# A row-wise infinity norm: 29 tail loads down to 704 columns in place of 25 down to 1152, two memsets behind them, early stores on ScalarE's queue

## Chip, cores, metric

Every program runs on one core of a Trainium2 chip. Time is device time in microseconds (us), the median of several executions. "Span" is the profiled execution from its first to its last instruction; the time lies about 1.8 us above it. A transfer has "landed" when the last of the sixteen updates of its semaphore is in the trace.

## The reference

```python
x = np.random.randn(8192, 8192).astype(np.float32)
def reference(x):
    return np.linalg.norm(x, ord=np.inf, axis=1)    # the largest |x| of each row
```

256 MiB are read once, 32 KiB are written.

## The kernel before

23 "big" loads of 128 partitions x 16384 columns (two rows a partition) fill a ring of three buffers; VectorE takes the largest magnitude of each row. The last 18 rows of every partition, the tail, come in shrinking loads, so that VectorE is soon done once the last byte is there. A planner, working backwards from the end, sizes them with two cost lines: a load costs `LOAD[0]` us a column and `LOAD[1]` a load, a reduction `REDUCE` likewise. Rows cut into several pieces are put together by GpSimd, the last row by the last reduction itself, which reads the partial maxima behind its own piece.

```python
LOAD = (1.1775e-3, 0.075)
REDUCE = (1.0417e-3, 0.060)
ROWS = 18
FIRST = 1152          # the last load's columns, at most
SNAP = 0.7
IDLE = 6
...
            fit = int((lag + slack - REDUCE[1] * n) / REDUCE[0])   # what VectorE can do in time
...
    for i in range(IDLE):
        tc.keep_in_program_order(nc.vector.memset(idle[:, i : i + 1], 0.0))

    early = nc.sync.dma_start(              # the 46 results a partition of the big loads
        out=out[:split].rearrange("(p q) -> p q", p=P), in_=res_big.rearrange("p t r -> p (t r)")
    )
    out_tail = out[split:].rearrange("(p r) -> p r", p=P)        # 18 results: 72 bytes a partition
    middle = nc.sync.dma_start(out=out_tail[:, : ROWS - 2], in_=res_tail[:, : ROWS - 2])
    for store in (early, middle):
        tc.add_manual_dep(store.ins, pieces.last[-2].name, ...)   # wait for the second-last reduction
    ...                                                           # SyncE waits for GpSimd
    last = nc.sync.dma_start(out=out_tail[:, ROWS - 2 :], in_=res_tail[:, ROWS - 2 :])
```

So there are three stores: the early one writes 184-byte runs, one a partition; the middle one the first 64 bytes of each 72-byte stretch of the tail's output; the last one the remaining 8 bytes of each stretch. The memsets write single elements that nothing reads.

Of the kernel before, what the change touches and what calls it, by code (L numbers as in the profile page):

```python
# [11 lines left out]
SEMS = 8  # L12


LOAD = (1.1775e-3, 0.075)
REDUCE = (1.0417e-3, 0.060)
ROWS = 18
FIRST = 1152
SNAP = 0.7
GRAIN = 64  # L20

IDLE = 6


def tail_loads(n_cols, big):







    slack = 0.0
    lag = REDUCE[0] * FIRST + REDUCE[1]
    loads = []
    end = ROWS * n_cols

    def take(top, bottom, most):
        nonlocal slack
        w = 0  # L40
        n = 0
        while True:

            n += 1
            start = max(bottom, (top - 1) // n_cols * n_cols - (n - 1) * n_cols)
            fit = int((lag + slack - REDUCE[1] * n) / REDUCE[0])
            w = max(w, min(fit, top - start) // GRAIN * GRAIN)
            if fit <= top - start or start <= bottom:
                break
        w = max(GRAIN, min(w, most, top - bottom))  # L50
        row = (top - w + n_cols - 1) // n_cols * n_cols
        if top - row >= SNAP * w or (w == most and top > row):
            w = top - row
        n = (top - 1) // n_cols - (top - w) // n_cols + 1
        slack += (LOAD[0] - REDUCE[0]) * w + LOAD[1] - REDUCE[1] * n
        loads.append((top - w, w))
        return top - w

    ends = [take(end, end - n_cols, FIRST), take(end - n_cols, end - 2 * n_cols, n_cols)]
    for top, bottom in zip(ends, (end - n_cols, 0)):  # L60
        while top > bottom:
            top = take(top, bottom, big)
    return loads[::-1]
# [61 lines left out]
def kernel(  # L125
# [5 lines left out]
    nc = tc.nc  # L131
# [3 lines left out]
    tail = tail_loads(n_cols, R * n_cols)  # L135
    split = n_rows - ROWS * P
    n_big = split // (R * P)
# [8 lines left out]
    res_big = single.tile([P, n_big, R], f32)  # L146
    res_tail = single.tile([P, ROWS], f32)
    idle = single.tile([1, IDLE], f32)
    pieces = Pieces(tc, ring)
# [9 lines left out]
    for i, (start, w) in enumerate(tail):  # L159
        c = 0  # L160
        while c < w:
            row = (start + c) // n_cols
            n = min(w - c, (row + 1) * n_cols - start - c)
            parts.append((row, i, c, n))
            c += n
    of_row = [[q for q in parts if q[0] == row] for row in range(ROWS)]

# [4 lines left out]
    for row, own in enumerate(of_row):  # L172
        if row == ROWS - 1:
            spots[own[-1][1]] = at
# [13 lines left out]
    for i, (start, w) in enumerate(tail):  # L188
# [8 lines left out]
        )  # L197
        for row in range(ROWS - 1):
            if len(of_row[row]) > 1 and of_row[row][-1][1] == i:
                best = dst[of_row[row][0]]  # L200
                more = [dst[q] for q in of_row[row][1:]]
                while more:
# [3 lines left out]
                        out=to,  # L206
# [7 lines left out]
    tc.declare_fence(done.ins, group="loads")  # L214
    for i in range(IDLE):
        tc.keep_in_program_order(nc.vector.memset(idle[:, i : i + 1], 0.0))  # L216

    early = nc.sync.dma_start(
        out=out[:split].rearrange("(p q) -> p q", p=P), in_=res_big.rearrange("p t r -> p (t r)")
    )  # L220
    out_tail = out[split:].rearrange("(p r) -> p r", p=P)
    middle = nc.sync.dma_start(out=out_tail[:, : ROWS - 2], in_=res_tail[:, : ROWS - 2])
    for store in (early, middle):
        tc.add_manual_dep(
            store.ins,
# [40 lines left out]
```

## Time and profile before

| | before |
|---|---|
| median of 3 runs | 629.24 us (629.21 to 629.35) |
| span | 627.395 us |
| first load landed | 22.556 us |
| last load landed | 623.594 us |
| last reduction | 623.715 to 625.062 us |
| last store issued, landed | 625.089, 626.550 us |

The profile's list of DMA issues gives the three stores, with KB and us from issue to landing:

```profile
out_dram<-res_big SPq DMA_DIRECT2D x1, 23.0 KB, 1.5
out_dram<-res_tail SPq DMA_DIRECT2D x1, 8.0 KB, 1.7
out_dram<-res_tail SPq DMA_DIRECT2D x1, 1.0 KB, 1.5
```

The 1 KB store that ends the kernel takes 1.5 us (1.461 in the trace).

### The profile page before, as it was taken

To read this page: it belongs to the slowest core of one execution; us is meant where nothing else is said; L and a number is where in the kernel's file an instruction comes from. 1 tells how busy PE (TensorE), PEld (TensorE's weight loads), DVE (VectorE), ACT (ScalarE), POOL (GpSimd) and SP (SyncE) were. 2 spreads that over 40 slices of the span, in tenths; PEclk is the share of its full clock that TensorE was granted. 3 is DMA by queue.
4 is the path that set the end of the run, shared out by engine and by line. 5 is a ranking of instruction groups with operands and counts; after the bars stand their busy time and mean duration, and the time that the engine had idled before them with its cause. 6 is when DMAs were issued, how large, how long until landed. Compare 5 with 4: busy or idle time off the path is not lost.

```text
span 627.4 us, 170 instructions
## 1 busy us (share of the span) xinstructions
DVE 551.9 (88%) x62; POOL 2.9 (0%) x13
## 2 busy tenths in 40 slices
DVE  0588988889988889888898888988889899999998
POOL 0000000000000000000000000000000000000000
DMA  9999999999999999999999999999999999999997
GB/s 401 401 468 401 468 401 468 401 468 401 468 401 468 401 468 401 468 401 468 401 468 401 468 401 464 405 455 414 443 410 440 452 401 429 432 440 429 419 423 298
DMA packets 7345, 268.48 MB, mean 428 GB/s; under 512 B 1200, under 2 KB 1200, under 8 KB 1968
## 3 DMA queue, kind: packets, MB, share of 16 engines
q1 hardware_dynamic: 7344, 268.47, 99.3%
q14 instruction: 1, 0.01, 0.0%
HBM read 268.44 MB, written 0.03 MB: 428 GB/s over the span
## 4 chain that ended last, share of the span: by engine, by line
DMA 57%; DVE 42%; issue 0%; DVEq 0%; SPq 0%
DMA ring<-in_x_dram 57%; DVE res_big L108 22%; DVE parts L108 11%; DVE res_tail L108 8%; DVE ring L108 1%; DVEq L261 0%; SPq L90 0%; DVE idle L216 0%
## 5 line engine op out<-in xcount | busy, mean ns | idle before, releaser
L108 DVE TENSOR_REDUCE res_big<-ring 128x2 f32<-128x16384 f32 x23 | 396.1, 17220 | 69.4 <-DMA ring<-in_x_dram 69.4
L108 DVE TENSOR_REDUCE res_tail<-ring 128x1 f32<-128x8192 f32 (+1 forms) x10 | 78.9, 7944 | 2.1 <-DMA ring<-in_x_dram 2.1
L108 DVE TENSOR_REDUCE parts<-ring 128x1 f32<-128x3520 f32 (+17 forms) x19 | 69.8, 3735 | 1.7 <-DMA ring<-in_x_dram 1.7
L108 DVE TENSOR_REDUCE ring<-ring 128x1 f32<-128x1984 f32 (+3 forms) x4 | 7.7, 1975 | 0.0
L205 POOL TENSOR_SCALAR res_tail<-parts 128x1 f32<-128x1 f32 x8 | 2.3, 289 | 614.1 <-DVE parts L108 614.1
L205 POOL TENSOR_SCALAR parts<-parts 128x1 f32<-128x1 f32 x1 | 0.4, 354 | 7.0 <-DVE parts L108 7.0
L250 POOL MEMSET const-bfloat16-1.0<- 128x1 bf16 x1 | 0.1, 102 | 0.0
L250 POOL MEMSET const-uint8-127<- 128x1 uint8 x1 | 0.1, 101 | 0.0
L250 POOL MEMSET const-float32-0.0<- 128x1 f32 x1 | 0.1, 98 | 0.2 <-issue 0.2
L250 POOL MEMSET const-float32-1.0<- 128x1 f32 x1 | 0.1, 98 | 0.0
L216 DVE MEMSET idle<- 1x1 f32 x6 | 0.1, 59 | 0.0
## 6 DMA issues: line engine op xcount, KB each, us to landing
ring<-in_x_dram SPq DMA_DIRECT2D x3, 4096.0 KB, 41.9
ring<-in_x_dram SPq DMA_DIRECT2D x1, 7488.0 KB, 31.1
ring<-in_x_dram SPq DMA_DIRECT2D x1, 6368.0 KB, 35.4
ring<-in_x_dram SPq DMA_DIRECT2D x1, 5920.0 KB, 40.8
ring<-in_x_dram SPq DMA_DIRECT2D x1, 4800.0 KB, 32.8
ring<-in_x_dram SPq DMA_DIRECT2D x1, 3488.0 KB, 40.4
ring<-in_x_dram SPq DMA_DIRECT2D x1, 3104.0 KB, 39.2
ring<-in_x_dram SPq DMA_DIRECT2D x1, 2944.0 KB, 40.8
```

The source lines that it names most:

```text
L108: ins = self.nc.vector.tensor_reduce(out=dst, in_=src, axis=mybir.AxisListType.X, op=mybir.AluOpType.max, apply_absolute_value=True,)
L205: combined = nc.gpsimd.tensor_scalar(out=to, in0=best, scalar1=two[0], scalar2=two[1] if len(two) == 2 else None, op0=mybir.AluOpType.max, ...
L216: tc.keep_in_program_order(nc.vector.memset(idle[:, i : i + 1], 0.0))
L250: nc = _bacc.Bacc("TRN2", target_bir_lowering=False, num_devices=1)
```

## The change

The intent: a smaller last piece leaves VectorE less to do after the last byte; 0.08 us are held back at each piece so that VectorE isn't late for it; and since the second-last reduction then ends only about 0.8 us before the last, the two early stores move to ScalarE's queue, out of the last store's way.

```diff
-LOAD = (1.1775e-3, 0.075)
+LOAD = (1.1775e-3, 0.073)
+SPARE = 0.08
-FIRST = 1152
-SNAP = 0.7
+FIRST = 768
+SNAP = 0.6
-IDLE = 6
+IDLE = 2
+        spare = SPARE if loads else 0
-            fit = int((lag + slack - REDUCE[1] * n) / REDUCE[0])
+            fit = int((lag + slack - spare - REDUCE[1] * n) / REDUCE[0])
-    early = nc.sync.dma_start(
+    early = nc.scalar.dma_start(
-    middle = nc.sync.dma_start(out=out_tail[:, : ROWS - 2], in_=res_tail[:, : ROWS - 2])
+    middle = nc.scalar.dma_start(
+        out=out_tail[:, : ROWS - 2], in_=res_tail[:, : ROWS - 2]
+    )
```

`FIRST` is only a cap. With 768 the planner's division comes out a hair under 768, and cut down to its grain of 64 columns that makes 704.

## The prediction

> **What bounds the kernel now.** I read the page first, then the timeline and the waits of the last microseconds, then three stretches of the tail.
>
> ```profile
> span 627.4 us, 170 instructions
> DVE 551.9 (88%) x62; POOL 2.9 (0%) x13
> DMA  9999999999999999999999999999999999999997
> q1 hardware_dynamic: 7344, 268.47, 99.3%
> HBM read 268.44 MB, written 0.03 MB: 428 GB/s over the span
> ...
> ring<-in_x_dram SPq DMA_DIRECT2D x1, 576.0 KB, 14.3
> ```
>
> The load queue is the bound: its packets fill 99.3% of 16 engines' span, and all 40 slices but the last read 9. VectorE works 88% of the span and is the follower. What can be won is the time between the last byte and the end, plus what every separate load costs the queue. The last line is the last load (1152 columns, 128 partitions, 4 bytes: 576 KB): it landed 14.3 us after its issue, so the queue held work and did not wait for issues.
>
> Next the waits of VectorE and the timeline from 615 us on (start, duration, what):
>
> ```profile
> DVE res_big L108 <- DMA ring<-in_x_dram: 69.4, 23, 22.6
> DVE parts L108 <- DMA ring<-in_x_dram: 1.7, 1, 1.7
> ```
>
> ```profile
> 622.32 1.47 DVE L108 TENSOR_REDUCE parts<-ring 128x1 f32<-128x1280 f32 x1
> 623.72 1.35 DVE L108 TENSOR_REDUCE res_tail<-ring 128x1 f32<-128x1156 f32 x1
> 623.82 0.35 SPq L218 DMA_DIRECT2D out_dram<-res_big  x1
> 623.97 0.28 POOL L205 TENSOR_SCALAR res_tail<-parts 128x1 f32<-128x1 f32 x1 [8.68 <-DVE parts L108]
> 624.21 0.43 SPq L222 DMA_DIRECT2D out_dram<-res_tail  x1
> 625.00 0.09 DVE L216 MEMSET idle<- 1x1 f32 x6
> 625.09 0.33 SPq L235 DMA_DIRECT2D out_dram<-res_tail  x1
> ```
>
> In the 23 big loads VectorE waits for each one. In the tail it waits once for 1.7 us (at 496.7 us) and never again: its reductions of shrinking pieces run back to back, a little behind the loads. The stretches say the same (us, busy and count by engine, clock, DMA share, GB/s):
>
> ```profile
> 564.00:600.00 36.00, 36.00 (x10) 1.12 (x4) 1.00 1.01 430
> 600.00:623.60 23.60, 23.60 (x11) 0.71 (x2) 1.00 0.97 404
> ```
>
> The trace's semaphore updates give the landings more finely than the page: the last load is complete at 623.594 us and the one before at 622.191. A reduction that finds VectorE free starts 0.024 us after the landing (22.556 to 22.580 for the first load). The last one started at 623.715, so it was 0.097 us late, behind VectorE's own work; the four before it were 0.09 to 0.11 us late too. The end is therefore: last landing 623.594, 0.121 to the start, 1.347 of reduction (to 625.062), 0.027 to the issue of the last store (625.089), 1.461 until that store has landed (626.550), and 0.845 of closing barriers to 627.395. The time of 629.24 lies 1.8 us over the span, which I take as fixed.
>
> **What the Trainium skill says.** "DMA: Bandwidth & Descriptors", section "Where 436 GB/s comes from", puts the ceiling of the 16 ports at 435.2 GB/s. I fitted the differences of the landings against the columns: 1.1764 ns a column plus 0.076 us a load, and all but the last load (0.028 us quicker) lie within 0.01 us of it. A column is 512 bytes, so the slope is 435.2 GB/s: the trace agrees, and the bytes cannot go faster; only the 0.076 us a load is open.
>
> "Perfetto Trace Analysis", section "Optimizing Scalar/DVE Operations", gives about 60 ns of overhead to a VectorE operation on SBUF and says that profiled latency is about twice this, since the write acknowledgement overlaps with the next instruction. The trace agrees: the step from the 1280-column reduction to the next is 1.394 us, that is 1.333 for 1280 columns at 1.0417 ns and 0.060 on top, while its listed duration is 1.474, 0.08 more.
>
> The DMA page's "Where the ~2 µs actually goes" puts most of a small transfer's fixed time into the write receipt. The last store's packets are over at 626.118 and its semaphore is full at 626.550, which fits. The same page's "Issuing engines are not separate DMA queues" says that another issuing engine saves only issue time. No run here shows that yet; I use it for ScalarE's stores.
>
> **The change, part by part.** I worked the new plan out with the fitted costs; the same arithmetic on the old plan puts the last reduction's end at 625.058 (measured 625.062).
>
> Four loads more (29 in place of 25), same bytes: 4 x 0.076 = +0.304 us on the bounding queue. The last landing goes from 623.594 to 623.898, keeping the 0.028 us that the last load was quicker.
>
> Smaller last piece: 704 columns and 6 partial maxima behind them, 710 elements in place of 1152 + 4 = 1156. 446 x 1.0417 ns = -0.465 us, so a duration of 0.882.
>
> The sparing term: the planner now takes 0.08 us off what VectorE may have at each piece behind the first, so that VectorE catches up. In my schedule the last reduction is 0.03 us late in place of 0.092 in the same model: -0.063 us. Sum at the end of the last reduction: 0.304 - 0.465 - 0.063 = -0.224, that is 624.83.
>
> The memsets, 6 to 2: the last store waits for the count that the last reduction gives, not for theirs. The semaphore's update comes 0.010 us after the reduction's end and the store starts 0.017 later, as after other reductions; the final update of the memsets comes at 625.128, after the store was issued. The page's wait of the last store for the memset is an inference from neighbouring times. Their updates are needed only at the closing drain, 1.5 us later: 0.00 us.
>
> The stores on ScalarE's queue: the second-last reduction (768 columns) should end at 624.03. Early and middle store, at their old distances from it, are issued at 624.06 and 624.45, the second taking 0.43 until 624.88. On SyncE that would hold up the last store, ready at 624.86, by some 0.05 us plus the instruction in between; on ScalarE it does not. So the move is worth nothing against before, and guards the 0.22 us of the rest. The middle store landed 1.72 us after its issue (624.214 to 625.933), so 626.17 now; the last one 624.86 + 1.461 = 626.32. The last store still ends last, by 0.15 us. The early store's packets would come at about 624.9, after the last load's 623.9, so they take nothing from the loads.
>
> Sum: 629.24 - 0.22 = 629.02.
>
> **The rivals.** First, the middle store becomes the end: its margin is 0.15 us. A first issue from ScalarE with 0.2 to 0.3 us more latency, or two stores side by side writing small runs into the same stretch of the output, would take it. For it: the middle store is already slower to land than the other two (1.72 against 1.47 and 1.46), and the two now start 0.4 apart in place of 0.875. Against it: their packets take only 0.2 us each. It would make 629.1 to 629.3.
>
> Second, VectorE stays behind: if each reduction costs 0.01 us more than I take, or the landings come a little sooner, the sparing term is eaten up over the last pieces, and the end is at the sum of reductions. That returns up to the 0.063, so 629.08. Against it: reductions of 1 to 2 thousand columns fit 1.0417 ns and 0.060 to 0.002 us.
>
> Third, the loads cost more when small: packets of 2816 bytes a partition in place of 4608. If the fixed cost of the five loads under 1280 columns were 0.1 in place of 0.076, the end moves by 0.12, to 629.14. Nothing in the loads down to 1280 columns hints at it; they keep the fit, and the 1152 one was quicker. If the missing 0.028 is a property of small loads and not of the last, the other four of these five would give 0.11 us more, and 628.91.
>
> **Range and chances.** All of these are tenths of a microsecond, 2% is 12.6. So "within 2%" is all but certain. I take 629.03, a shade above the sum for the first rival, and 628.86 to 629.28 as the range: from the friendly end of the third rival to the first rival at its worst. The spread of the three runs of before is 0.14 us, so a gain of 0.2 may be seen but hardly in a single run.
>
> **What would show it.** Last landing at 623.9; the last reduction of 710 elements lasting 0.88 and ending at 624.83; a start no more than 0.06 us behind its landing; small waits of VectorE for loads in the last ten pieces, where there were none; SyncE's last store issued 0.03 us after the reduction's end; ScalarE's middle store landing before it. I am wrong if the last landing is past 624.1 (loads dearer), if VectorE still shows no wait (spare eaten), or if the closing wait is ended by a ScalarE store.

## The result and the profile after

| | before | after |
|---|---|---|
| median, same rounds | 629.30 us (629.20 to 629.50, 6 runs) | 629.61 us (629.26 to 629.75, 6 runs) |
| ratio | | 1.0004, 95% interval 0.9991 to 1.0017 |

The ratio is the mean time of the changed kernel's fast runs over that of the other's of the same rounds, so it is not quite the ratio of the medians. "The same" by any 2% measure, as forecast, but the median lies 0.33 us above the top of the forecast range and on the other side of before: +0.31 where -0.22 was expected.

From the page after:

```profile
span 627.7 us, 175 instructions
q1 hardware_dynamic: 7632, 268.44, 99.3%
q10 hardware_dynamic: 288, 0.03, 0.0%
HBM read 268.44 MB, written 0.03 MB: 428 GB/s over the span
```

q10 is ScalarE's queue with the two early stores; the loads still fill 99.3%. The timeline from 622 us on answers the one in the prediction:

```profile
622.40 1.08 DVE L110 TENSOR_REDUCE ring<-ring 128x1 f32<-128x896 f32 x1
623.39 0.94 DVE L110 TENSOR_REDUCE parts<-ring 128x1 f32<-128x768 f32 x1
624.25 0.89 DVE L110 TENSOR_REDUCE res_tail<-ring 128x1 f32<-128x710 f32 x1
624.37 0.38 ACTq L220 DMA_DIRECT2D out_dram<-res_big  x1
624.51 0.36 POOL L207 TENSOR_SCALAR res_tail<-parts 128x1 f32<-128x1 f32 x1 [10.81 <-DVE parts L110]
624.79 0.51 ACTq L224 DMA_DIRECT2D out_dram<-res_tail  x1
625.08 0.06 DVE L218 MEMSET idle<- 1x1 f32 x2
625.16 0.35 SPq L239 DMA_DIRECT2D out_dram<-res_tail  x1
```

The last reduction takes 0.89 us, as computed, but ends at 625.14 where 624.83 was expected. The stores after, from the list of DMA issues:

```profile
out_dram<-res_big ACTq DMA_DIRECT2D x1, 23.0 KB, 2.1
out_dram<-res_tail ACTq DMA_DIRECT2D x1, 8.0 KB, 1.8
out_dram<-res_tail SPq DMA_DIRECT2D x1, 1.0 KB, 1.7
```

In this trace all three land more slowly than before, the deciding one by 0.2 us. And the very first reduction of the two traces (before, then after):

```profile
22.58 17.22 DVE L108 TENSOR_REDUCE res_big<-ring 128x2 f32<-128x16384 f32 x1 [22.58 <-DMA ring<-in_x_dram]
```

```profile
22.88 17.22 DVE L110 TENSOR_REDUCE res_big<-ring 128x2 f32<-128x16384 f32 x1 [22.88 <-DMA ring<-in_x_dram]
```

The same first load landed 0.30 us later, long before anything that the change touches. The difference of the spans, 627.678 - 627.395 = +0.283 us, is thus three pieces:

| piece | before | after | difference |
|---|---|---|---|
| first load's landing | 22.556 | 22.851 | +0.295 |
| from there to the end of the last reduction | 602.506 | 602.286 | -0.220 |
| from there to the end of the span ("tail" in the tables, not to be taken for the tail rows) | 2.333 | 2.541 | +0.208 |

The middle piece is what the prediction worked out (-0.224). The last one gives it back. The first needs a test: chance, or the price of a second queue?

### The profile page after: what moved, and what is told of

It reads as the page before. It is cut to its first block, busy times and chain, and to the rows that moved or that the text cites. A ratio compares the mean times of both kernels' runs of the same rounds, so it can differ in the third digit from the quotient of the medians.

```text
span 627.7 us, 175 instructions
## 1 busy us (share of the span) xinstructions
DVE 552.1 (88%) x62; POOL 3.2 (1%) x14
## 3 DMA queue, kind: packets, MB, share of 16 engines
q1 hardware_dynamic: 7632, 268.44, 99.3%
## 4 chain that ended last, share of the span: by engine, by line
DMA 57%; DVE 42%; issue 0%; DVEq 0%; SPq 0%
DMA ring<-in_x_dram 57%; DVE res_big L110 22%; DVE parts L110 12%; DVE res_tail L110 7%; DVE ring L110 1%; DVEq L265 0%; SPq L92 0%; DVE idle L218 0%
## 5 line engine op out<-in xcount | busy, mean ns | idle before, releaser
L110 DVE TENSOR_REDUCE parts<-ring 128x1 f32<-128x3136 f32 (+18 forms) x22 | 78.5, 3633 | 1.2 <-DMA ring<-in_x_dram 1.2
L110 DVE TENSOR_REDUCE res_tail<-ring 128x1 f32<-128x8192 f32 (+1 forms) x9 | 69.8, 7811 | 2.1 <-DMA ring<-in_x_dram 2.1
L110 DVE TENSOR_REDUCE ring<-ring 128x1 f32<-128x1600 f32 (+5 forms) x6 | 8.3, 1444 | 0.0
```

The costliest lines, as they stand in the source:

```text
L110: ins = self.nc.vector.tensor_reduce(out=dst, in_=src, axis=mybir.AxisListType.X, op=mybir.AluOpType.max, apply_absolute_value=True,)
```

## The experiments

Theory A: the gain at the last reduction is real and is given back because the last store lands slowly when other stores are close in front of it; the late start is chance. Theory B: using ScalarE's queue delays the start of the load stream. Rivals C (two queues at once make the receipts slow) and D (the plan of 29 loads, or the two memsets, do) came with them.

Fifteen kernels were run, each with five timed runs beside nine of before, and one trace. In the table, F is the first load's landing, R the end of the last reduction; "last store" is from issue to landing; all from the trace, in us. Span minus F is the time with the chance of the start taken out.

| run | F | R - F | last store | tail | span - F | median | before, same rounds |
|---|---|---|---|---|---|---|---|
| before | 22.556 | 602.506 | 1.461 | 2.333 | 604.839 | | |
| after | 22.851 | 602.286 | 1.669 | 2.541 | 604.827 | 629.61 | 629.30 |
| after_again | 22.549 | 602.300 | 1.919 | 2.792 | 605.092 | 629.45 | 629.15 |
| sp_stores | 22.554 | 602.281 | 1.702 | 2.806 | 605.087 | 629.24 | 629.15 |
| act_only | 22.573 | 602.540 | 1.415 | 2.286 | 604.826 | 629.19 | 629.15 |
| no_middle | 22.690 | 602.299 | 1.510 | 2.363 | 604.662 | 629.17 | 629.15 |
| late_stores | 22.469 | 602.473 | 2.021 | 2.894 | 605.367 | 629.42 | 629.32 |
| fifo | 22.638 | 602.290 | 1.404 | 2.275 | 604.565 | 628.99 | 629.32 |
| act_early | 22.659 | 602.346 | 1.435 | 2.308 | 604.654 | 629.09 | 629.32 |
| idle6 | 22.442 | 602.269 | 1.788 | 2.661 | 604.930 | 629.20 | 629.32 |
| early_close | 22.586 | 602.273 | 1.498 | 2.370 | 604.643 | 629.17 | 629.23 |
| fifo_before | 22.558 | 602.711 | 1.430 | 2.304 | 605.015 | 629.30 | 629.23 |
| nospare | 22.525 | 602.340 | 1.747 | 2.620 | 604.960 | 629.20 | 629.23 |
| fifo_tuned | 22.584 | 602.698 | 1.407 | 2.284 | 604.982 | 629.44 | 629.23 |
| middle_close | 22.419 | 602.390 | 1.627 | 2.501 | 604.891 | 629.11 | 629.25 |
| elsewhere | 22.544 | 602.264 | 1.454 | 2.327 | 604.591 | 628.92 | 629.25 |
| fifo_no_middle | 22.544 | 602.306 | 1.644 | 2.498 | 604.804 | 629.15 | 629.25 |

Every ratio to before has 1 inside its 95% interval (about plus or minus 0.0013), so no time alone settles a tenth of a microsecond; the terms of the traces do the work.

### The start, and the two queues

**after_again** is the changed kernel unaltered.

> The changed kernel unaltered, to see what repeats. Theory A (gain at the last reduction, given back by the stores; the start is chance): from the first load's landing to the end of the last reduction 602.29 us again (602.51 before), last store 1.67 us from issue to landing again (1.46 before), but the first load's landing somewhere between 22.5 and 22.9 us by chance, so that the median against before is within 0.2 us. Theory B (using ScalarE's queue delays the start of the load stream): the first landing is again near 22.85, and the kernel is again 0.3 us slower.

F was 22.549, not 22.85: the late start did not repeat, and with it the sign that theory B named is gone. The reduction's end repeated to 0.014 us. The last store was slower still, 1.919. So, with a normal start, the tail alone took back 0.46 us where 0.21 had been gained; the median was again 0.30 above before.

**act_only** is the kernel before with the two early stores on ScalarE's queue.

> The kernel before with early and middle store on ScalarE's queue, nothing else. Theory A: the last store starts 0.87 us behind the middle one as before, so its landing takes 1.46 to 1.5 us and the time is that of before within 0.1 us. Theory B: first landing near 22.85 and 0.3 us slower than before. Rival C: last store near 1.67 us, 0.2 us slower than before.

```diff
-    early = nc.sync.dma_start(
+    early = nc.scalar.dma_start(
-    middle = nc.sync.dma_start(
+    middle = nc.scalar.dma_start(
```

```profile
out_dram<-res_tail SPq DMA_DIRECT2D x1, 1.0 KB, 1.4
```

F 22.573, last store 1.415 us, 0.847 us behind the middle one's issue: theories B and C both fail, and A holds, with a store somewhat quicker than the 1.46 to 1.5 that it named. Over all 17 traces F lies between 22.419 and 22.851, with a median of 22.556, and the 11 kernels with ScalarE's queue are on both sides of it (their own median is 22.549). The first trace of the changed kernel happened to be the latest of them. The six traces without that queue lie closer together, from 22.544 to 22.638; whether the second queue widens the scatter is not shown.

**sp_stores** puts both early stores of the changed kernel back on SyncE.

```diff
-    early = nc.scalar.dma_start(
+    early = nc.sync.dma_start(
-    middle = nc.scalar.dma_start(
+    middle = nc.sync.dma_start(
```

> The changed kernel with early and middle store back on SyncE's queue. Theory A: the last store is issued about 0.05 to 0.1 us later than in the changed kernel and its landing still suffers from the neighbours (1.6 us), so the tail from the last reduction's end stays at 2.5 to 2.6 us, against 2.33 before; time within 0.15 us of the changed kernel. Theory B: first landing back at 22.55 and 0.3 us faster than the changed kernel. Rival C (the slow receipts come from two queues at once): last store back to 1.46 us.

The timeline shows what ScalarE's queue is good for:

```profile
623.95 0.88 DVE L110 TENSOR_REDUCE res_tail<-ring 128x1 f32<-128x710 f32 x1
624.06 0.35 SPq L220 DMA_DIRECT2D out_dram<-res_big  x1
624.46 0.52 SPq L224 DMA_DIRECT2D out_dram<-res_tail  x1
...
625.10 0.36 SPq L239 DMA_DIRECT2D out_dram<-res_tail  x1
```

The last store goes out 0.26 us after the reduction's end (624.835), in place of 0.03: SyncE is still issuing the middle one. That delay of 0.23 was expected at 0.05 to 0.1. Even so the last store, now 0.64 us behind the middle one, took 1.702 us: one queue is no cure, so rival C fails here too. Nor did the move to ScalarE pay as a whole: the tail of 2.806, above the 2.5 to 2.6 that was expected, lies close to the changed kernel's second trace (2.792), and the median of 629.24 is below its 629.45, within the scatter.

### Is it the neighbours?

**late_stores** gives the kernel before the same close stores: 25 loads and six memsets, but the early stores held back so that the middle one starts only 0.4 us ahead of the last.

```diff
 # act_only, and:
-            pieces.last[-2].name,
+            combined.ins.name,        # GpSimd's last combine
```

> The kernel before (25 loads, six memsets) with early and middle store on ScalarE's queue and held back until GpSimd's last combine, so that they start 0.4 us later and the last store follows the middle one by 0.4 to 0.45 us as in the changed kernel, in place of 0.85. Theory A (the last store's landing is slowed by neighbours that are still landing): last store 1.65 us or more from issue to landing, against 1.42 in the run with ScalarE's queue alone; tail from the last reduction's end 2.5 us or more; 0.2 us slower than before. Rival D (the slow landing belongs to the plan of 29 loads or to the two memsets): last store stays at 1.42 to 1.5 us and the time at that of before within 0.1.

```profile
623.57 1.38 DVE L108 TENSOR_REDUCE res_tail<-ring 128x1 f32<-128x1156 f32 x1
...
624.58 0.45 ACTq L222 DMA_DIRECT2D out_dram<-res_tail  x1
624.88 0.07 DVE L216 MEMSET idle<- 1x1 f32 x6
624.97 0.35 SPq L235 DMA_DIRECT2D out_dram<-res_tail  x1
```

```profile
out_dram<-res_tail SPq DMA_DIRECT2D x1, 1.0 KB, 2.0
```

2.021 us, against 1.415 in act_only, with the same loads and the same queue. Rival D, the plan of loads, falls; the neighbours are enough. The traced run (629.62) is one of the longer of its five, and the median was only 0.10 above before where 0.2 was expected, so 2.021 may be at the high end.

**no_middle** leaves the middle store out; the last store takes all 18 columns.

```diff
-    middle = nc.scalar.dma_start(
-        out=out_tail[:, : ROWS - 2], in_=res_tail[:, : ROWS - 2]
-    )
-    for store in (early, middle):
+    for store in (early,):
-    last = nc.sync.dma_start(out=out_tail[:, ROWS - 2 :], in_=res_tail[:, ROWS - 2 :])
+    last = nc.sync.dma_start(out=out_tail, in_=res_tail)
```

> The changed kernel without the middle store: the last store takes all 18 columns of the tail. Theory A: with only the early store in front of it, the last store lands in 1.45 to 1.55 us, tail from the last reduction's end 2.33 to 2.4 us, 0.1 to 0.2 us faster than the changed kernel. If instead a 72-byte run takes as long as the middle store's 64-byte run (1.72 us before), nothing is won and the size of the runs, not the neighbour, sets the landing.

1.510 us and a tail of 2.363, as theory A had it; span minus F is 0.177 below before.

**fifo** keeps all three stores but issues the two early ones on SyncE right behind the last load, where their packets stand in line after its packets; **act_early** lets them go from ScalarE as soon as their data are there.

```diff
 # fifo: sp_stores, and (act_early: the changed kernel, and)
-    for store in (early, middle):
-        tc.add_manual_dep(store.ins, pieces.last[-2].name, ...)
```

> The changed kernel with early and middle store on SyncE's queue right behind the last load's issue, with no wait on the second-last reduction. Their packets stand in the queue behind those of the last load. Theory A: both have landed by about 625.2 us, before the last store's packets; last store 1.45 to 1.5 us, tail 2.33 us, so 0.2 us faster than before and 0.2 to 0.4 faster than the changed kernel. If the last load's landing is delayed by their packets (0.2 us), the first landing to the end of the last reduction goes from 602.29 to 602.4 to 602.5. Rival D: last store still 1.65 us or more.

> The changed kernel with early and middle store still on ScalarE's queue but with no wait on the second-last reduction: the early one goes out when the big reductions are done (about 467 us), the middle one when row 15 is combined (about 608 us). Theory A: last store 1.45 us, tail 2.33 us, and 0.1 to 0.2 us lost on the loads beside which the 256 small packets run: 602.4 to 602.5 us from the first landing to the end of the last reduction, so the time of before within 0.1 us, or 0.1 better. Rival D: last store still 1.65 us or more.

In fifo both stores had landed by 624.315, and the last one stands alone (timeline, then its issue in the list of DMA issues):

```profile
624.03 0.89 DVE L110 TENSOR_REDUCE res_tail<-ring 128x1 f32<-128x710 f32 x1
...
624.96 0.33 SPq L231 DMA_DIRECT2D out_dram<-res_tail  x1
```

```profile
out_dram<-res_tail SPq DMA_DIRECT2D x1, 1.0 KB, 1.4
```

The last store took 1.404 us, R - F was 602.290, span minus F 604.565: 0.274 less than before. Here the whole predicted gain arrives, plus 0.06 from a last store quicker than before's. The medians are 628.99 against 629.32; the five runs (628.88 to 629.14) and the nine of before (629.11 to 629.47) barely touch. In act_early the last store took 1.435 us. Its R - F is 0.05 to 0.06 above the changed kernel's two traces, less than the expected loss to the packets that ran beside the loads; middle_close, below, has 602.390 although no store packets run there before its last load, so even this may be scatter.

**idle6** is the changed kernel with six memsets.

```diff
-IDLE = 2
+IDLE = 6
```

> The changed kernel with six memsets in place of two. The prediction said that the memsets are off the path: last store issued 0.03 us after the last reduction's end as with two, landing 1.65 us or more as in the changed kernel, time within 0.15 us of it. Rival D: if the memsets shape the end, last store back to 1.45 us and 0.2 us faster.

The last store was issued 0.028 us after the reduction's end, as with two, and took 1.788 us, between the 1.669 and 1.919 of the changed kernel's two traces. The memsets are off the path.

### Which property of the neighbour?

Three kernels on the plan of 29 loads place one store, alone, so that its packets end just as the last store's begin. **early_close** does it with the early store, and has the middle one behind the last load; **middle_close** the reverse; **elsewhere** is middle_close with the middle store's 64-byte runs sent to another part of the output, which makes the result wrong.

```diff
 # middle_close: the changed kernel, and
-    early = nc.scalar.dma_start(
+    early = nc.sync.dma_start(
-    for store in (early, middle):
+    for store in (middle,):
-            pieces.last[-2].name,
+            combined.ins.name,
 # early_close: with middle and early exchanged.  elsewhere: middle_close, and
-        out=out[:split].rearrange("(p q) -> p q", p=P), in_=res_big.rearrange("p t r -> p (t r)")
+        out=out[:split].rearrange("(p q) -> p q", p=P)[:, ROWS - 2 :],
+        in_=res_big.rearrange("p t r -> p (t r)")[:, ROWS - 2 :],
-        out=out_tail[:, : ROWS - 2], in_=res_tail[:, : ROWS - 2]
+        out=out[:split].rearrange("(p q) -> p q", p=P)[:, : ROWS - 2],
+        in_=res_tail[:, : ROWS - 2],
```

> The changed kernel with the middle store out of the way behind the last load, and the early store held back until GpSimd's last combine, so that it (and it alone) is still landing when the last store's packets come. Reading A1 (any store close in front slows the last one's landing): last store 1.6 us or more from issue to landing. Reading A2 (it takes the middle store, whose runs lie in the same 72-byte stretches of the output): last store 1.4 to 1.5 us. The early store itself may land last, near 626.2 to 626.4 us.

> The changed kernel with the early store out of the way behind the last load, and the middle store on ScalarE's queue held back until GpSimd's last combine, so that it alone is still landing when the last store's packets come. Reading A2 (same stretches of the output): last store 1.65 us or more. Reading A3 (it takes the whole pile of stores, early and middle together): last store 1.4 to 1.5 us, as with the early store alone.

> As middle_close, but the middle store's 64-byte runs go to the first 16 columns of the early part of the output, which the early store leaves out (the result is wrong on purpose: 16 columns hold the wrong rows' values and the tail's first 16 are not written). Reading A2: last store back to 1.4 to 1.5 us, 0.2 us or more quicker than in middle_close. If the mere nearness of a store of 64-byte runs does it: 1.65 us or more, as in middle_close.

middle_close and elsewhere have the same timeline to 0.01 us (the last line of each is from the list of DMA issues):

```profile
624.58 0.37 ACTq L224 DMA_DIRECT2D out_dram<-res_tail  x1
624.75 0.06 DVE L218 MEMSET idle<- 1x1 f32 x2
624.84 0.34 SPq L239 DMA_DIRECT2D out_dram<-res_tail  x1
out_dram<-res_tail SPq DMA_DIRECT2D x1, 1.0 KB, 1.6
```

```profile
624.58 0.38 ACTq L225 DMA_DIRECT2D out_dram<-res_tail  x1
624.75 0.06 DVE L218 MEMSET idle<- 1x1 f32 x2
624.84 0.34 SPq L241 DMA_DIRECT2D out_dram<-res_tail  x1
out_dram<-res_tail SPq DMA_DIRECT2D x1, 1.0 KB, 1.5
```

The last store took 1.627 us in the first and 1.454 in the second; early_close gave 1.498. The medians of the same rounds are 629.11 and 628.92. With equal issue times, run sizes and queues of the two close stores, the place that the neighbour writes makes 0.17 us. (In elsewhere the new place also has its 64-byte runs 184 bytes apart in place of 72; against spacing as the cause speaks early_close, whose 184-byte runs lie without gaps and which is nearly as quick.) It was not quite the "0.2 us or more", and 1.627 misses the "1.65 or more" by a hair; but the order is as reading A2 has it, and A3 (only the pile of both) fails. Each landing is one trace; the changed kernel itself scattered from 1.669 to 1.919, so the size of the effect is known roughly, its direction better.

Set side by side, the traces also say where the time goes. From issue to the end of its own packets, the last store took 1.02 to 1.06 us in all 17. What differs is the rest, until the last of its sixteen semaphore updates:

| 8-byte last store | traces | from its last packet to landing | of its 16 updates, later than 1.5 us after issue |
|---|---|---|---|
| nine or more of the 16 updates of a middle store to the same stretches still missing when its first packet starts | after, after_again, sp_stores, late_stores, idle6, nospare, middle_close | 0.59 to 0.98 us | 5 to 10 |
| none to two of them missing, or the middle store elsewhere | before, act_only, fifo, act_early, early_close, fifo_before, fifo_tuned, elsewhere | 0.38 to 0.46 us | none |

The groups do not overlap, and each of the four chips has traces in both. So the cause of the slow landing is shown, down to the place that is written; why writes to the same stretches hold each other up is not.

**fifo_no_middle** was to be the version that follows: the early store behind the last load, no middle store.

```diff
 # no_middle, and
-    early = nc.scalar.dma_start(
+    early = nc.sync.dma_start(
-    for store in (early,):
-        tc.add_manual_dep(store.ins, pieces.last[-2].name, ...)
```

> The changed kernel with the early store right behind the last load and no middle store: the last store takes all 18 columns alone. From the first landing to the last reduction's end 602.29 us, last store 1.40 to 1.51 us, tail 2.27 to 2.38: 0.15 to 0.3 us faster than before, about as the version with both stores behind the last load (628.99 where before had 629.32).

A miss: the single store of 72-byte runs took 1.644 us with nothing near it, so the gain was only 0.035 in span minus F. Fifteen of its sixteen updates were there by 1.482 us, as in no_middle (1.499); a single late one made the difference, and why it was late is open. Of the versions that compute the reference, fifo stays the best.

### The terms of the load plan

**nospare** sets the sparing term to zero.

```diff
-SPARE = 0.08
+SPARE = 0.0
```

> The changed kernel with the sparing term at 0 (still 29 loads down to 704, other pieces up to 64 columns wider). My schedule gives 602.35 us from the first landing to the end of the last reduction, 0.07 more than the changed kernel, with the last reduction starting 0.10 us late in place of 0.03. If the term is worth nothing: 602.29.

R - F was 602.340, about 0.05 above the changed kernel's 602.286 to 602.300, and the last reduction started 0.112 us later than a free VectorE would have (0.030 and 0.048 in the changed kernel's traces). By this one trace the term is worth about 0.05; the schedule had said 0.07.

**fifo_before** gives the kernel before the stores of fifo (the wait on `pieces.last[-2]` taken out, nothing else), and **fifo_tuned** tries a smaller last piece.

```diff
 # fifo_tuned: fifo, and
-LOAD = (1.1775e-3, 0.073)
-SPARE = 0.08
-FIRST = 768
-SNAP = 0.6
+LOAD = (1.1764e-3, 0.076)
+SPARE = 0.02
+FIRST = 576
+SNAP = 2.0
```

> The kernel before (25 loads, down to 1152) with both early stores right behind the last load on SyncE's queue. It separates the plan of loads from the place of the stores: first landing to the end of the last reduction 602.5 us as before, last store 1.40 to 1.46, tail 2.27 to 2.33, so at most 0.06 us faster than before, and 0.2 us slower than the 29 loads with the same place of the stores.

> A try for a version that beats both: both early stores right behind the last load, and the planner with the measured costs of a load (1.1764 ns a column and 0.076 us), a last piece of 576 columns, a sparing term of 0.02 us and no snapping to rows. My schedule gives 602.12 us from the first landing to the end of the last reduction (602.29 in the changed kernel); with a tail of 2.28 us it would be 0.35 to 0.4 us faster than before.

Both missed, in R - F. In fifo_before the last load's packets ended as early as before (623.153 against 623.143), but its semaphore was full only 0.736 us later, not 0.45; in fifo that distance was 0.51. The other kernels have 0.43 to 0.54, so that of fifo is nothing special, and only fifo_before's stands out, by at least 0.2. Whether the store packets right behind the load held it up stays open. In fifo_tuned one load of 5312 columns took 0.544 us more than the fitted cost, and all five timed runs were long (629.35 to 629.80), so it is hardly chance; why stays open too. No part of the argument about the changed kernel rests on either.

## Why the prediction was wrong

**The bound and the loads: right.** Four loads at 0.076 us were to move the last landing by 0.304. From first to last landing the traces give 601.038 us before and 601.329 and 601.366 after: +0.29 and +0.33. The third rival, dearer small loads, did not come: those of 768 to 1152 columns lie within 0.01 us of the fit in both traces, and only the last load was again quicker, by about 0.05. (The fit itself is a little looser than stated: before, the step to the second load is 0.021 off.)

**The last reduction: right.** Forecast 0.882 us for 710 elements, measured 0.885 and 0.880. The sum of loads, last piece and sparing was -0.224 at the end of the last reduction; measured from the first landing it was -0.220 and -0.206. One sign named in the prediction did not show: VectorE never waited for a load in the last pieces; it was merely less late (0.097 us before, 0.048 and 0.030 after). That VectorE shows no wait had been named as a sign of being wrong, and so had a last landing past 624.1; in the first trace it came at 624.180. Both signs showed without their reason: the sparing term was not eaten up, and the landing was late only by the start. One line was misread: in the tail VectorE waited twice for a load, 2.1 us at the first tail piece and 1.7 us at 496.7, not once; nothing rests on it.

**Memsets and ScalarE's queue: right in kind.** The last store left 0.028 us after the reduction, with two memsets as with six. On SyncE it would have left 0.26 us after it, more than the 0.05 and an instruction that were forecast.

**The step that failed: "the last one 624.86 + 1.461".** The last store's landing was carried over from the kernel before as if it were a constant. It was 1.669 and 1.919 us in the changed kernel, because the change lets the last store follow the middle one by 0.38 us in place of 0.875, while that one is still landing on the same stretches of the output. What grew is the part behind its last packet, from 0.44 us to 0.63 and 0.88. The prediction had looked at this part and taken it for most of a fixed time ("which fits"); that does not fit, since it is 0.43 of 1.461 us, and it is the part that is not fixed. The first rival named the circumstance ("two stores side by side writing small runs into the same stretch", started 0.4 us apart) but read it as a danger for the middle store ending last, behind a margin of 0.15 us. The middle store did land first in both traces, but in the first one only because the last store was slowed: at 1.461 us that one would have landed 0.01 us behind it. late_stores made the old plan's last store slow by that means alone, fifo took it from the new plan and got the gain.

**The range.** The tail's +0.208 and +0.459 set against -0.22 make -0.01 and +0.25 us; this is span minus F of the two traces against before, 604.827 and 605.092 against 604.839. The medians are +0.31 and +0.30. The rest of the first is not shown, as only one run of each call has a trace: the chance of the start, which spans 0.43 us over 17 traces and made +0.295 in the first one, is large enough. The range had no term for a last store of another length, and it had taken the 0.14 us of three runs for the scatter; the six of before then spread over 0.30 and those after over 0.49.

## What to carry to other kernels

A small store's time from issue to landing is not a constant of the store: see what else is landing close by, above all in the same stretch of memory, before carrying it into a sum. Results that are ready early can go out early, where they run behind the last load instead of in front of the last store; this paid in fifo, while in fifo_before that load landed late and nothing was won. When a change moves tenths of a microsecond, take the start's chance out by measuring from the first landing, and compare terms of traces, not medians.

## What the Trainium skill lacked or had wrong

- "DMA: Bandwidth & Descriptors" has no figure for what two small stores close together in time and place cost each other. Here a 1 KB store of 8-byte runs landed in 1.627 us behind a store to the same 72-byte stretches, in 1.454 behind the same store to another place, and in up to 2.021 behind a pile of two. The page's "Specifications" give a read-modify-write for transfers under 512 B; that would fit, but no run here shows it.
- The same page puts a fixed cost of about 2 us on a DMA by itself, for those that GpSimd issues. What one load more costs a queue that is never empty is not there: 0.076 us each, from the landings of the 48 loads of the kernel before.
- The same page, "Issuing engines are not separate DMA queues", calls the saved issue time usually small beside the transfer. It agrees in kind (sp_stores was no quicker to land), but at the end of a kernel it was 0.23 us of a 1.7 us store.
- No page tells of the scatter at the start: the first 8 MB load landed between 22.419 and 22.851 us in 17 traces of kernels that begin alike.
